# Order of the first loads, of the second unit's weight split and of the first gate recurrences in a hybrid block kernel

## The chip, the cores and the metric

The kernel runs on one core of a Trainium2 chip. The metric is the device time of one execution in microseconds (us), as a median of runs. A core has five engines with a queue of instructions each, executed in order: TensorE (PE, with its weight loads shown apart as PEld), VectorE (DVE), ScalarE (ACT), GpSimd (POOL) and SyncE (SP), which here issues nearly all transfers (DMAs).

## What is computed

One layer of a hybrid block on 16 meta tokens and 2048 tokens of width 1024, all in float32:

```python
h = concatenate([meta, x])                       # 2064 x 1024
p = rms_norm(h, norm_mix_pre) @ w_in             # 1024 -> 512 + 1544 + 1024 columns
oa = rg_lru_group(...)                           # a gated linear recurrence
ob = forgetting_attention_group(q, k, v, f_logit, fox_f_bias)
oc = rwkv7_group(...)                            # a matrix-valued recurrence
h = h + rms_norm(concatenate([oa, ob, oc]) @ w_out, norm_mix_post)
f = causal_dwconv(rms_norm(h, norm_ffn_pre) @ ffn_up)
h = h + rms_norm((gelu(gate) * val) @ ffn_down, norm_ffn_post)
```

The attention's decay comes from eight gate columns of p: `log_f = log_sigmoid(f_logit + f_bias)` and `c = cumsum(log_f)` along the tokens. That cumulative sum is the gate recurrence of the title.

## The kernel before

Each float32 product is made of three matmuls on rounded parts: an operand x becomes hi (rounded by ACT) and lo = x - hi (by DVE), and `mm3` (lines 185 to 189) adds hi*hi, hi*lo and lo*hi. So weights and tokens alike pass through a cast on ACT and a subtraction on DVE before PE can use them.

The input projection goes first. `w_in_part` (L334) takes the tokens in three parts of two blocks each; the first block of the first part has 400 tokens (the 16 meta tokens and three tiles of 128), the second 384 (three tiles). `w_in_norm` (L202) calls `norm_transpose` (L133) for each tile: a load on SP (L137), the sum of squares on ACT (L124), a scalar on DVE (L127), its power -0.5 on POOL (L128), the product with the reciprocal root and the norm's scale `g_pre` on DVE (L142), then eight transposes on PE into two PSUM tiles `pst` (L155), a cast to `xh` on ACT (L161) and a subtraction to `xl` on DVE (L162) for each. In the first part the second block's tiles are turned between the first units' products (`core.turn_tile`).

A unit is 128 output columns. Its weights (`wh`, `wl`) are loaded raw and split: L239 to L241 for the first two units, L177 to L182 for the others; two units' weights fit at a time (pool `w`), and the halves are stored (L250) for the later parts. For a block a unit costs 24 matmuls into one PSUM tile `psp`, evacuated by ACT (L58) or DVE (L60) to `stp` and stored (L277). Ahead of the units come the eight gate columns, 16 matmuls for a block into `psf` (L323, L324), evacuated at L326 and L328 and stored to `scr_f` (L329).

`gate_block` (L445) reads `scr_f` back (L457) and makes the cumulative sum: Abs, Exp and Ln on ACT (L459 to L461, with loads of ACT's function table between), DVE steps and the scan (L462 to L470), a cast on ACT (L475), a subtraction on DVE (L476) and two stores (L477, L478). It is the first step of `recurrences` (L2177), which a helper (`Beside`) advances between the units from the fourteenth unit on. The gated recurrences of the other two groups follow it, then attention, the output projection, and the up and down projections of the feed-forward.

The kernel is written in program order, and a scheduler sets the order of each engine's queue from priorities and its own model of time. `tc.issue_after(ins)` is an order edge: the instructions traced in its block stand behind `ins` on `ins`'s engine, with no semaphore. So code that stands late in the program can come early in a queue: the first `gate_block` stands behind thirteen units in the program, and its first load was placed right behind the store of `scr_f`.

Of the kernel before, what the change touches and what calls it, by code (L numbers as in the profile page):

```python
# [8 lines left out]
F32 = mybir.dt.float32  # L9
# [4 lines left out]
ALU = mybir.AluOpType  # L14
# [4 lines left out]
P = 128  # L19
# [13 lines left out]
class Core:  # L33


    def __init__(self, tc, ctx):
        self.tc = tc
        self.nc = tc.nc
        self.ctx = ctx
        self.uid = 0  # L40
        nc = self.nc
        self.const = ctx.enter_context(tc.tile_pool(name="const", bufs=1))
        self.ident = self.const.tile([P, P], F32, name="ident")
        make_identity(nc, self.ident[:])
        self.flip = 0
        self.root = self.apart = False
        self.power = None
        self.turns = 0

    def n(self, s):  # L50
# [79 lines left out]
    return rstd_from(core.nc, v, ss, width, core.apart)  # L130


def norm_transpose(core, pools, psum, src, rows, gain, pieces, after=nullcontext):  # L133

    nc = core.nc
    xt = pools["nt"].tile([P, D], F32, tag="nt_x", name=core.n("xt"))
    nc.sync.dma_start(xt[:rows], src)  # L137
    junk = pools["st"].tile([P, D], BF16, tag="stv", name=core.n("xj"))
    v = pools["nt"].tile([P, 6], F32, tag="rs", name=core.n("rs"))
    with after():  # L140
        rs = rstd_of(core, v[:rows], xt[:rows], D, junk[:rows])
    nc.vector.scalar_tensor_tensor(xt[:rows], xt[:rows], rs, gain[:rows], op0=ALU.mult, op1=ALU.mult)  # L142
    transpose_split(core, psum, xt, rows, pieces)


def transpose_split(core, psum, xt, rows, pieces):

    nc = core.nc
    for k0 in range(0, KD, 4):
        ps = psum.tile([P, 4, P], F32, tag="mm", name=core.n("pst"))
        for k in range(4):
            nc.tensor.transpose(  # L155
                ps[:, k, :rows], xt[:rows, (k0 + k) * P : (k0 + k + 1) * P], core.ident[:rows, :rows]
            )
        ks = slice(k0, k0 + 4)
        for hi, lo, c, r0, n in pieces:
            ds_, ss_ = slice(c, c + n), slice(r0, r0 + n)  # L160
            nc.scalar.activation(hi[:, ks, ds_], ps[:, :, ss_], AF.Copy)  # L161
            nc.vector.tensor_tensor(lo[:, ks, ds_], ps[:, :, ss_], hi[:, ks, ds_], op=ALU.subtract)  # L162


def split_load(core, pool, raws, src, shape, tag):
# [65 lines left out]
    return scr["wk"][c0 // P]  # L231


def w_in_weights(core, pools, w_in, c0, scr, part, raw=None):

    src = w_in[:, c0 : c0 + P].rearrange("(k p) c -> p k c", p=P)
    if raw is not None:
        pair = hi, lo = [pools["w"].tile([P, KD, P], F32R, tag=s, name=core.n(s)) for s in ("wh", "wl")]
        core.loaded = core.nc.sync.dma_start(raw, src)  # L239
        core.rounded = core.nc.scalar.activation(hi[:], raw, AF.Copy)  # L240
        core.nc.vector.tensor_tensor(lo[:], raw, hi[:], op=ALU.subtract)  # L241
    elif part == 0:
        pair = split_load(core, pools["w"], (pools["nt"], "nt_x", None), src, [P, KD, P], "w")
    else:
        core.turns += part == 2
        pl, tags = (pools["nt"], ("nt_x", "nt_x")) if core.turns % 4 > 1 else (pools["w"], ("wh", "wl"))
        pair = [pl.tile([P, KD, P], F32R, tag=tag, name=core.n(s)) for s, tag in zip(("wh", "wl"), tags)]
    for t, kept in zip(pair, w_in_kept(scr, c0)):
        t = t[:].rearrange("p k c -> p (k c)").bitcast(F32)
        core.loaded = core.nc.sync.dma_start(*((kept, t) if part == 0 else (t, kept)))  # L250
    return pair
# [82 lines left out]
def w_in_part(core, pools, psum, w_in, blocks, scr, part):  # L334
# [12 lines left out]
    if part == 0:  # L347
        raws = pools["rp"].tile([P, 2, KD, P], F32, tag="rw_e", name=core.n("raw"))
        firsts = [
            (w_in_weights(core, pools, w_in, c0, scr, part, raws[:, i]), kind, c0)  # L350
            for i, (kind, c0) in enumerate(units[:2])
        ]
        for i, block in enumerate(blocks):
# [91 lines left out]
def gate_block(core, R, f_bias, scr, tl):  # L445
# [8 lines left out]
        return R.t([NH, 400], s, dt)[:, :n]  # L454

    x = new("k")
    nc.sync.dma_start(x, scr["f"][:, t0 : t0 + n])  # L457
    a = new("r")
    nc.scalar.activation(a, x, AF.Abs, bias=core.fb[:])  # L459
    nc.scalar.activation(a, a, AF.Exp, scale=-1.0)  # L460
# [1741 lines left out]
def hybrid_block_kernel(ctx: ExitStack, tc: tile.TileContext, args, out):  # L2202
# [12 lines left out]
    def pool(es, name, bufs, **kw):  # L2215
        return es.enter_context(tc.tile_pool(name=name, bufs=bufs, **kw))
# [11 lines left out]
    with ExitStack() as p1:  # L2228
# [7 lines left out]
        rp = pool(rec, "rp", 1, **right)  # L2236
        with ExitStack() as p1a:
            ps_mm = pool(p1a, "ps_mm", 5, space=PSUM)
            g_pre = spread(pool(p1a, "gpre", 1), a["norm_mix_pre"], "g_pre")
            pools = {"xn": pool(p1a, "xn", 1), "nt": pool(p1a, "nt", 4), "w": pool(p1a, "w", 2), "st": pool(p1a, "st", 2)}  # L2240
            pools["us"], pools["rp"] = pool(p1a, "us", 1), rp
            sums = up_sums(core, pools["us"], a["ffn_up"], scr, EARLY)
            split_out = w_out_split(core, pools["nt"], a["w_out"], scr)
            core.power = core.const.tile([P, 1], F32, name="power")
            nc.vector.memset(core.power[:], -0.5)
            following = w_in_norm(core, pools, ps_mm, x, meta, g_pre, 0)
            for part in range(3):
                blocks = following
                units = w_in_part(core, pools, ps_mm, a["w_in"], blocks, scr, part)
                for i in range(READY if part == 0 else 0):  # L2250
                    while not next(units):
                        pass
                    if i == 4:
                        begun = core.loaded.ins
                if part == 0:
                    zeros = pools["st"].tile([P, PAD], F32, tag="sth", name="zeros")
                    nc.vector.memset(zeros[:], 0.0)
# [4 lines left out]
                        attn_consts(core)  # L2262
                    shared, core.const = core.const, rc
                    p1c = ExitStack()
                    p1c.enter_context(tc.issue_after(begun))
# [238 lines left out]
```

## Time and profile before

| | |
|---|---|
| median of 3 runs | 2953.49 us (2950.68 to 2956.22) |
| the profiled execution | 2962.62 us, its span 2960.9 us |
| PE busy | 2844.5 us, 96% of the span |
| DVE, ACT, POOL busy | 2002.2, 1505.8, 1297.3 us |
| mean granted TensorE clock | 0.976 |

The profile shows one execution, so sums are made against its own 2962.62 us. Times in it are microseconds from the start of the span. "Idle before <- releaser" is the time in which an engine had nothing to run, and what ended it. Tile names carry no numbers there; in listings of the program's order they do.

### The profile page before, as it was taken

Reading aid. Unit: us, or ns where it says so; the run is one execution under the profiler, and the core shown is the slowest. Engines: PE = TensorE matmul, PEld = TensorE weight load, DVE = VectorE, ACT = ScalarE, POOL = GpSimd, SP = SyncE. Lnnn points to the kernel's source line nnn. Section 1 sums busy time; section 2 is a strip of 40 time slices with the busy share of each in tenths; the row PEclk is TensorE's granted clock in tenths of the full one; section 3 lists DMA queues with packets and bytes.
Section 4 is the critical chain, followed back from the end, with each engine's and each line's share of the span. In section 5 each row is a group of like instructions: output and inputs, shape, how many; then the busy total and the mean of one; then the engine's idle time right before and its main releaser. Section 6 shows DMA issues by size and latency. Waiting matters only on the chain.

```text
span 2960.9 us, 53225 instructions
## 1 busy us (share of the span) xinstructions
PE 2844.5 (96%) x18854; PEld 2448.4 (83%) x18854; DVE 2002.2 (68%) x3839; ACT 1505.8 (51%) x2937; POOL 1297.3 (44%) x1572
## 2 busy tenths in 40 slices
PE   7998999999978889999999999999999999999998
PEld 7997989989865555566578999999999999787887
DVE  4257654666578765556656998888777787646766
ACT  4236442554346655555635666666566665324333
POOL 1002221222114667666723667355655544656443
PEclk9999999999988999999999999999999999999999
DMA  6776678577653357435255665577777774436453
GB/s 218 248 245 203 198 249 290 166 245 234 203 126 73 87 127 222 108 102 139 58 158 173 209 188 174 164 234 207 215 202 224 218 197 141 146 116 218 149 171 121
DMA packets 470343, 530.51 MB, mean 179 GB/s; under 512 B 86862, under 2 KB 356888, under 8 KB 468524
## 3 DMA queue, kind: packets, MB, share of 16 engines
q1 hardware_dynamic: 469308, 526.18, 58.9%
q8 instruction: 148, 2.42, 0.3%
q0 software_dynamic: 768, 0.93, 0.1%
q14 instruction: 119, 0.97, 0.1%
HBM read 368.07 MB, written 158.90 MB: 178 GB/s over the span
## 4 chain that ended last, share of the span: by engine, by line
PE 69%; DVE 7%; ACT 6%; DMA 5%; issue 2%; POOL 2%; SPq 1%; DVEq 0%; ACTq 0%; POOLq 0%
PE psu L187 9%; PE psu L188 9%; PE psu L189 9%; PE po L779 4%; PE psd L187 4%; PE psd L188 4%; PE psd L189 4%; PE psp L187 2%; PE psp L189 2%; PE psp L188 2%; PE sc L756 2%; PE mx L627 2%; PE sc L757 2%; PE pswo L187 2%; PE pswo L188 2%
## 5 line engine op out<-in xcount | busy, mean ns | idle before, releaser
L188 PE MATMUL psu<-xo,uw 128*128 128x344 f32 x1848 | 591.5, 320 | 0.0
L187 PE MATMUL psu<-xo,uw 128*128 128x344 f32 x1848 | 585.8, 322 | 3.3 <-ACT u L1933 2.3
L189 PE MATMUL psu<-xo,uw 128*128 128x344 f32 x1848 | 582.0, 320 | 0.3 <-DVE uw L1762 0.2
L187 PE MATMUL psp<-xh,wh 128*128 128x384 f32 (+2 forms) x1152 | 383.0, 333 | 0.4 <-DVE rww L1462 0.3
L188 PE MATMUL psp<-xl,wh 128*128 128x384 f32 (+2 forms) x1152 | 378.3, 328 | 0.0
L189 PE MATMUL psp<-xh,wl 128*128 128x384 f32 (+2 forms) x1152 | 375.6, 326 | 0.0
L1762 DVE TENSOR_TENSOR uw<-uq,uw 128x512 fp32r<-128x512 f32 x341 | 319.0, 940 | 60.6 <-ACT uw L1761 57.5
L187 PEld LDWEIGHTS psu<-xo,uw 128*128 128x128 f32 x1848 | 345.8, 188 | 4.8 <-ACT u L1933 2.6
L188 PEld LDWEIGHTS psu<-xo,uw 128*128 128x128 f32 x1848 | 347.1, 188 | 0.0
L189 PEld LDWEIGHTS psu<-xo,uw 128*128 128x128 f32 x1848 | 345.7, 188 | 1.2 <-DVE uw L1762 1.1
L1761 ACT ACTIVATE uw<-uq 128x512 fp32r<-128x512 f32 x462 | 288.1, 627 | 98.1 <-PE psu L189 41.1
L761 ACT ACTIVATE p<-sc,bias 128x512 f32<-128x512 f32 (+4 forms) x352 | 196.8, 590 | 164.3 <-PE sc L757 134.9
L632 DVE TENSOR_REDUCE mc<-mx 128x1 f32<-128x512 f32 (+5 forms) x352 | 191.8, 565 | 113.6 <-PE mx L627 83.7
L1901 DVE SCALAR_TENSOR_TENSOR uy<-psu,ffn_cols,uy 128x342 f32<-128x342 f32 (+1 forms) x390 | 220.5, 567 | 61.1 <-ACT uy L1899 59.7
L1909 POOL TENSOR_TENSOR uy<-uy,uy 128x342 f32<-128x342 f32 (+1 forms) x132 | 145.8, 1105 | 230.6 <-DVE uy L1901 58.4
L1762 POOL TENSOR_TENSOR uw<-uq,uw 128x512 fp32r<-128x512 f32 x121 | 183.3, 1515 | 133.7 <-ACT uw L1761 111.5
L187 PEld LDWEIGHTS psp<-xh,wh 128*128 128x128 f32 x1152 | 220.4, 191 | 7.7 <-issue 4.4
L188 PEld LDWEIGHTS psp<-xl,wh 128*128 128x128 f32 x1152 | 220.5, 191 | 5.6 <-issue 3.9
L189 PEld LDWEIGHTS psp<-xh,wl 128*128 128x128 f32 x1152 | 220.3, 191 | 4.3 <-issue 3.0
L800 POOL TENSOR_TENSOR acc<-acc,p 128x512 f32<-128x512 f32 (+3 forms) x186 | 196.4, 1059 | 49.8 <-DVE acc L800 22.2
L1762 DVE TENSOR_TENSOR fo<-u,fo 128x896 fp32r<-128x896 f32 x88 | 102.0, 1159 | 130.0 <-ACT fo L1761 129.4
L1761 ACT ACTIVATE fo<-u 128x896 fp32r<-128x896 f32 x88 | 81.2, 923 | 205.9 <-PE psd L189 118.3
(492 smaller groups left out, 6289.8 us busy)
## 6 DMA issues: line engine op xcount, KB each, us to landing
uq<-scr_us SPq DMA_DIRECT2D x220, 256.0 KB
uq<-in_ffn_up_dram SPq DMA_DIRECT2D x209, 256.0 KB
wl<-scr_wk SPq DMA_DIRECT2D x48, 512.0 KB
wh<-scr_wk SPq DMA_DIRECT2D x48, 512.0 KB
u<-scr_ff SPq DMA_DIRECT2D x88, 256.0 KB
scr_ff<-uy SPq DMA_DIRECT2D x110, 171.0 KB
raw<-in_w_in_dram SPq DMA_DIRECT2D x24, 512.0 KB
scr_wk<-wh SPq DMA_DIRECT2D x24, 512.0 KB
```

The costliest lines, as they stand in the source:

```text
L187: nc.tensor.matmul(out, ah, bh, start=first, stop=False, skip_group_check=more)
L188: nc.tensor.matmul(out, ah, bl, start=False, stop=False, skip_group_check=more)
L189: nc.tensor.matmul(out, al, bh, start=False, stop=last, skip_group_check=more)
L627: nc.tensor.matmul(ps[:rows, : e - a], q3[:, qo : qo + rows], k2[:, a:e], start=True, stop=not last)
L632: self.reduced = nc.vector.tensor_reduce(mc[:rows, i, ci : ci + 1], ps[:rows, : e - a], axis=AX.X, op=ALU.max)
L761: last = nc.scalar.activation(p[:rows, :w], ps[:rows, :w], AF.Exp, bias=bias[:rows, j : j + 1])
L779: mm = nc.tensor.matmul(po[at : at + 64, c0:n], v1[:rows, j], p[:rows, : n - c0], start=start and i < 2, stop=end and i + 2 >= len(group), ...
L800: eng.tensor_tensor(a, ps_[0][0][:rows, c0:n] if start and i == 1 else a, p[:rows, : n - c0], op=ALU.add)
L1761: core.nc.scalar.activation(hi, src, AF.Copy)
L1762: (eng or core.nc.vector).tensor_tensor(lo, src, hi, op=ALU.subtract)
L1901: core.conved = stt(y[:, :n], src[:, i : n + i], cw[:, 44 * i + cc : 44 * i + cc + 1], y[:, :n], op0=ALU.mult, op1=ALU.add)
L1909: core.pooled = nc.gpsimd.tensor_tensor(v[:, :n], g[:, :n], v[:, :n], op=ALU.mult)
```

## The change

It has three parts. The loads of the meta tokens and of the first full tile are issued ahead of the load of `g_pre`: they are kept in `core.held`, from which `norm_transpose` takes them. The second unit's cast and subtraction are put behind the last `xh` cast and the last `xl` subtraction traced before them (`core.high`, `core.low`), which are those of the first block's last tile. And the load of `gate_block` is put behind `core.begun`, the last store of weights traced in the fifth turn (i = 4) of the first part's loop; that name held the constants' edge before, as `begun`.

```diff
-        self.power = None
+        self.power, self.held = None, []
...
+def token_load(core, pools, src, rows):
+
+    xt = pools["nt"].tile([P, D], F32, tag="nt_x", name=core.n("xt"))
+    core.nc.sync.dma_start(xt[:rows], src)
+    return xt
...
 def norm_transpose(core, pools, psum, src, rows, gain, pieces, after=nullcontext):
-    xt = pools["nt"].tile([P, D], F32, tag="nt_x", name=core.n("xt"))
-    nc.sync.dma_start(xt[:rows], src)
+    xt = core.held.pop(0) if core.held else token_load(core, pools, src, rows)
...
-            nc.scalar.activation(hi[:, ks, ds_], ps[:, :, ss_], AF.Copy)
-            nc.vector.tensor_tensor(lo[:, ks, ds_], ps[:, :, ss_], hi[:, ks, ds_], op=ALU.subtract)
+            core.high = nc.scalar.activation(hi[:, ks, ds_], ps[:, :, ss_], AF.Copy)
+            core.low = nc.vector.tensor_tensor(lo[:, ks, ds_], ps[:, :, ss_], hi[:, ks, ds_], op=ALU.subtract)
...
-def w_in_weights(core, pools, w_in, c0, scr, part, raw=None):
+def w_in_weights(core, pools, w_in, c0, scr, part, raw=None, behind=False):
-        core.rounded = core.nc.scalar.activation(hi[:], raw, AF.Copy)
-        core.nc.vector.tensor_tensor(lo[:], raw, hi[:], op=ALU.subtract)
+        with core.tc.issue_after(core.high.ins) if behind else nullcontext():
+            core.rounded = core.nc.scalar.activation(hi[:], raw, AF.Copy)
+        with core.tc.issue_after(core.low.ins) if behind else nullcontext():
+            core.nc.vector.tensor_tensor(lo[:], raw, hi[:], op=ALU.subtract)
...
-            (w_in_weights(core, pools, w_in, c0, scr, part, raws[:, i]), kind, c0)
+            (w_in_weights(core, pools, w_in, c0, scr, part, raws[:, i], i > 0), kind, c0)
...
     x = new("k")
-    nc.sync.dma_start(x, scr["f"][:, t0 : t0 + n])
+    with core.tc.issue_after(core.begun):
+        nc.sync.dma_start(x, scr["f"][:, t0 : t0 + n])
...
-            g_pre = spread(pool(p1a, "gpre", 1), a["norm_mix_pre"], "g_pre")
+            gpre = pool(p1a, "gpre", 1)
...
+            core.held = [token_load(core, pools, meta, META), token_load(core, pools, x[:P, :], P)]
+            g_pre = spread(gpre, a["norm_mix_pre"], "g_pre")
             following = w_in_norm(core, pools, ps_mm, x, meta, g_pre, 0)
...
                     if i == 4:
-                        begun = core.loaded.ins
+                        core.begun = core.loaded.ins
```

What the edges do to the queues is read from the program's order (line, operation, tiles with their numbers, shape; the lines of the changed kernel are higher by 6 to 11). DVE's queue in the opening, before: `pst_165` to `pst_216` belong to the first block's three full tiles, `wl_232` and `wl_239` to the first and second unit, `fw` to the gate columns.

```order
L142 SCALAR_TENSOR_TENSOR xt_201<-xt_201,rs_204,g_pre 128x1024
L241 TENSOR_TENSOR wl_232<-raw_230,wh_231 128x1024
L162 TENSOR_TENSOR xl_132<-pst_165,xh_131 128x4x128
L241 TENSOR_TENSOR wl_239<-raw_230,wh_238 128x1024
L162 TENSOR_TENSOR xl_132<-pst_172,xh_131 128x4x128
L315 TENSOR_TENSOR fw_223<-fraw_224,fw_223 128x8x8
L162 TENSOR_TENSOR xl_132<-pst_187,xh_131 128x4x128
L127 TENSOR_SCALAR rs_298<-rs_298 128x1
L162 TENSOR_TENSOR xl_132<-pst_194,xh_131 128x4x128
L162 TENSOR_TENSOR xl_132<-pst_209,xh_131 128x4x128
L162 TENSOR_TENSOR xl_132<-pst_216,xh_131 128x4x128
```

The same place of DVE's queue in the changed kernel:

```order
L168 TENSOR_TENSOR xl_136<-pst_165,xh_135 128x4x128
L148 SCALAR_TENSOR_TENSOR xt_201<-xt_201,rs_204,g_pre 128x1024
L249 TENSOR_TENSOR wl_232<-raw_230,wh_231 128x1024
L168 TENSOR_TENSOR xl_136<-pst_172,xh_135 128x4x128
L168 TENSOR_TENSOR xl_136<-pst_187,xh_135 128x4x128
L168 TENSOR_TENSOR xl_136<-pst_194,xh_135 128x4x128
L127 TENSOR_SCALAR rs_298<-rs_298 128x1
L323 TENSOR_TENSOR fw_223<-fraw_224,fw_223 128x8x8
L168 TENSOR_TENSOR xl_136<-pst_209,xh_135 128x4x128
L168 TENSOR_TENSOR xl_136<-pst_216,xh_135 128x4x128
L148 SCALAR_TENSOR_TENSOR xt_295<-xt_295,rs_298,g_pre 128x1024
L249 TENSOR_TENSOR wl_239<-raw_230,wh_238 128x1024
```

`wl_239` has moved from the middle to behind the last `xl` and the next tile's product; the first tile's `xl` has moved ahead of the last tile's product. On ACT, `wh_238` moved likewise, and the square of the fifth tile (`xt_295`) now stands ahead of the casts of `pst_209` and `pst_216`.

ACT's queue at the second block's tiles (`pst_303` to `pst_382`), before, with the first gate's operations on `rwr_1343` and `rwk_1352`:

```order
L161 ACTIVATE xh_133<-pst_310 128x4x128
L459 ACTIVATE rwr_1343<-rwk_1341,fb 8x400
L460 ACTIVATE rwr_1343<-rwr_1343 8x400
L461 ACT_TABLE_LOAD
L461 ACTIVATE rwr_1343<-rwr_1343 8x400
L475 ACTIVATE rwk_1352<-rwsq_1349 8x400
L161 ACTIVATE xh_133<-pst_353 128x4x128
L161 ACTIVATE xh_133<-pst_360 128x4x128
L161 ACTIVATE xh_133<-pst_375 128x4x128
L161 ACTIVATE xh_133<-pst_382 128x4x128
L326 ACTIVATE fa_406<-psf_389 8x384
```

In the changed kernel those operations stand further on in ACT's queue, between the weights of the sixth unit (`wh_659`) and of the seventh (`wh_723`):

```order
L187 ACTIVATE wh_659<-raw_661 128x1024
L468 ACTIVATE rwr_1343<-rwk_1341,fb 8x400
L58 ACTIVATE stp_628<-psp_603 128x400
L469 ACTIVATE rwr_1343<-rwr_1343 8x400
L470 ACT_TABLE_LOAD
L470 ACTIVATE rwr_1343<-rwr_1343 8x400
L484 ACTIVATE rwk_1352<-rwsq_1349 8x400
L187 ACTIVATE wh_723<-raw_725 128x1024
```

The casts of `pst_353` to `pst_382` now follow that of `pst_310` directly. On SP the gate's load stands behind the store of `wh_659`; the second gate's operations moved from behind the third unit's weights to behind the seventh's. PE's order is the same in both programs up to the start of the attention.

More of the change, by code (lines that the diff above doesn't have):

```diff
@@ L2264, in hybrid_block_kernel @@
                     p1c = ExitStack()
-                    p1c.enter_context(tc.issue_after(begun))
+                    p1c.enter_context(tc.issue_after(core.begun))
                     p1c.enter_context(tc.issue_after(core.powered.ins))
```

## The prediction

> **What bounds the kernel now.** I began with the head of the page: TensorE (PE) is busy nearly throughout, so a gain has to be time in which PE waits or runs on a slow clock.
>
> ```profile
> span 2960.9 us, 53225 instructions
> PE 2844.5 (96%) x18854; PEld 2448.4 (83%) x18854; DVE 2002.2 (68%) x3839; ACT 1505.8 (51%) x2937; POOL 1297.3 (44%) x1572
> ```
>
> Then the busy time by stretches. A row gives start:end and length, then busy us (and instructions) of PE, PEld, DVE, ACT, POOL, then the granted TensorE clock, the DMA share and GB/s.
>
> ```profile
> 36.76:38.63 1.87, 0.00 (x1) 0.00 (x0) 1.87 (x5) 1.87 (x5) 0.00 (x0) 1.00 0.16 52
> 39.20:42.30 3.10, 3.08 (x10) 2.70 (x9) 0.95 (x2) 0.00 (x0) 0.00 (x0) 0.50 1.04 268
> 42.60:200.00 157.40, 157.40 (x879) 153.94 (x879) 52.58 (x117) 47.84 (x79) 9.29 (x15) 1.00 0.76 249
> 900.00:1100.00 200.00, 175.55 (x1677) 112.20 (x1675) 149.76 (x424) 120.65 (x264) 119.52 (x193) 0.88 0.38 90
> 1700.00:2500.00 800.00, 799.90 (x5080) 799.20 (x5079) 648.71 (x1001) 504.60 (x994) 434.65 (x343) 1.00 0.67 197
> ```
>
> From 42.6 us PE is the bound without a gap, at full clock; so is the up projection at 1700 to 2500. Time can be won before 42.6 us, and whatever is won there reaches 200 us whole. The stretch at 900 to 1100, where attention runs beside the last recurrences, is the soft one: 24.45 us idle, mean clock 0.88. Third, what PE waits for in the first 75 us (waits in total, times, longest):
>
> ```profile
> PE pst L155 <- DVE xt L142: 9.1, 2, 8.9
> PE psf L323 <- ACT xh L161: 3.2, 2, 1.9
> PE psf L324 <- DVE xl L162: 0.6, 1, 0.6
> ```
>
> So the opening is bound by DVE and ACT, which norm, transpose and split the tokens; PE follows them.
>
> **First tokens ahead of the norm's scale.** The timeline of the opening (start, length, engine, line, tiles, and in brackets the idle time before and its releaser):
>
> ```profile
> 0.81 0.39 SPq L2223 DMA_DIRECT2D g_pre<-in_norm_mix_pre_dram  x1
> 5.53 1.05 ACT L124 ACTIVATE xj<-xt 16x1024 bf16<-16x1024 f32 x1 [3.44 <-DMA xt<-in_meta_tokens_dram]
> 7.54 1.27 DVE L142 SCALAR_TENSOR_TENSOR xt<-xt,rs,g_pre 16x1024 f32<-16x1024 f32 x1 [0.56 <-POOL rs L128]
> 7.99 1.06 ACT L124 ACTIVATE xj<-xt 128x1024 bf16<-128x1024 f32 x1 [1.31 <-DMA xt<-in_x_dram]
> 9.34 1.06 ACT L124 ACTIVATE xj<-xt 128x1024 bf16<-128x1024 f32 x1 [0.21 <-DMA xt<-in_x_dram]
> 9.99 1.28 DVE L142 SCALAR_TENSOR_TENSOR xt<-xt,rs,g_pre 128x1024 f32<-128x1024 f32 x1 [0.67 <-POOL rs L128]
> ```
>
> The squares of the first two full tiles follow their loads and start 9.34 - 7.99 = 1.35 us apart: one 512 KB transfer. The scale g_pre is as large, so with it behind, the meta tokens and the first tile land about 1.35 us earlier. But L142 reads the scale too, and that now lands where the first tile used to, near 7.9. So the meta tile's L142 moves from 7.54 to about 7.95 (later), and the first tile's follows 1.27 us behind at 9.2 in place of 9.99: 0.75 us earlier. The third and fourth tiles do not land sooner, since the bytes ahead of them are the same. I take 0 for this edit alone; its ends are -0.4 (the later scale) and +0.75 us.
>
> **Second unit's weights behind the first block's tiles.** What PE's dense work waits for:
>
> ```profile
> 16.32 1.22 DVE L241 TENSOR_TENSOR wl<-raw,wh 128x1024 fp32r<-128x1024 f32 x1
> 18.84 1.87 DVE L162 TENSOR_TENSOR xl<-pst,xh 128x512 fp32r<-128x512 f32 x3
> 20.17 0.70 PE L324 MATMUL psf<-xl,fw 128*128 128x400 f32 x1 [0.55 <-DVE xl L162]
> ```
>
> The first L324 needs xl of all four tiles; PE goes on without a gap once it starts at 20.17. DVE is busy for 10.23 of the 10.7 us ahead of it,
>
> ```profile
> 10.00:20.70 10.70, 6.65 (x28) 5.11 (x29) 10.23 (x17) 9.21 (x19) 1.65 (x3) 0.91 1.00 292
> ```
>
> so an operation taken out of its queue shows in full. The second unit's L241 (1.22 us) goes behind the last xl, and its L240 (ACT) behind the last xh. Against it, the square of the fifth tile now stands ahead of the last two xh, which costs ACT one square (1.06 us) at about the price of the cast that left. The weights are first used when the second unit starts, some ten microseconds later; that is their cover. Gain 1.2 us, ends 0 (ACT becomes the later one) and 2.0 (with the 0.75 above).
>
> **First gates' recurrence behind unit five.** Around the second block's tiles:
>
> ```profile
> 30.32 0.28 SPq L457 DMA_DIRECT2D rwk<-scr_f  x1
> 31.86 0.63 ACT L459 ACTIVATE rwr<-rwk,fb 8x400 f32<-8x400 f32 x1 [0.53 <-DMA rwk<-scr_f]
> 33.08 1.28 ACT L461 ACT_TABLE_LOAD   x1
> 34.85 1.91 PE L155 MATMUL pst<-ident,xt 128*128 128x128 f32 x16
> 36.62 0.54 ACT L475 ACTIVATE rwk<-rwsq 8x400 fp32r<-8x400 f32 x1 [1.71 <-DVE rwsq L470]
> 37.06 2.00 ACT L161 ACTIVATE xh<-pst 128x512 fp32r<-128x512 f32 x4
> 37.68 2.47 DVE L162 TENSOR_TENSOR xl<-pst,xh 128x512 fp32r<-128x512 f32 x4
> 38.63 0.44 PE L323 MATMUL psf<-xh,fw 128*128 128x384 f32 x1 [1.87 <-ACT xh L161]
> 39.60 0.69 PE L324 MATMUL psf<-xl,fw 128*128 128x384 f32 x1
> 42.62 0.34 PE L189 MATMUL psp<-xh,wl 128*128 128x384 f32 x1
> ```
>
> The four xh casts stand behind L475 on ACT, which waits for the scan on DVE. PE's sixteen transposes end at 36.76, and PE idles 1.87 us. Without the gate on ACT the casts follow the transposes: the first group of four is there at 34.85 + 1.91/4, about 35.4; the casts are 0.5 us apart (2.00/4), so the third, for which L323 waits, ends near 36.9 and L323 starts near 37.0. Then xl is late next: 0.62 apart (2.47/4) on DVE, the third ends near 38.0, where L324 stood at 39.60. That is 1.6 us; I take 1.5, ends 0 and 1.87.
>
> The second part is the clock. It was 1.00 while PE idled and 0.50 in 39.20 to 42.30. From 39.60 to 42.62 PE started nine matmuls in 3.02 us; at the pace of the next stretch (157.40 / 879 = 0.179 us each) they take 1.61. The wait left over is a few tenths, so I count the slow stretch as gone: 1.4 us, ends 0 and 1.4.
>
> [...]
>
> ```profile
> 11.33 1.57 PEld L155 LDWEIGHTS pst<-ident,xt 128*128 128x128 f32 x8 [1.54 <-DVE xt L142]
> 16.45 0.42 PEld L155 LDWEIGHTS pst<-ident,xt 128*128 128x128 f32 x4 [0.81 <-DVE xl L162]
> ```
>
> **The gate's new place.** Its load now stands on SP behind the store of the sixth unit's wh, and L459 on ACT behind that cast, ahead of one stp and the seventh unit's wh:
>
> ```profile
> 75.67 0.38 SPq L250 DMA_DIRECT2D scr_wk<-wh  x1
> 77.56 1.06 ACT L181 ACTIVATE wh<-raw 128x1024 fp32r<-128x1024 f32 x1 [2.40 <-PE psp L188]
> 86.15 1.06 ACT L181 ACTIVATE wh<-raw 128x1024 fp32r<-128x1024 f32 x1 [1.51 <-PE psp L188]
> 34.37 0.54 ACT L461 ACTIVATE rwr<-rwr 8x400 f32<-8x400 f32 x1
> 34.95 0.56 DVE L463 TENSOR_TENSOR rwk<-rwk,rwr 8x400 f32<-8x400 f32 x1 [2.01 <-ACT rwr L461]
> 35.55 1.04 DVE L470 TENSOR_TENSOR_SCAN rwsq<-ones,ctail,rwk 8x400 f32<-8x400 f32 x1
> 691.81 4.76 DMA rwk<-scr_f
> ```
>
> With the opening 4.1 us ahead, the load goes out near 72.0 and lands 1.5 later (30.32 to 31.86) at 73.5. Then in line: L459 0.63, a stp 0.5 (like an xh cast), an exponential 0.54 (like the logarithm L461), the table load 1.28, the logarithm 0.54, L463 and L470 on DVE 1.6, L475 0.54, the cast 1.06 and the seventh unit's wl 1.2: 81.4. PE starts that unit when it frees the slot for the next cast, 86.15 - 4.1 = 82.05. So it is covered by about 0.7 us, and I price it at nothing. If the load takes the 4.76 us that a later gate's load takes in the chain that ended last (the last row), PE waits 4.76 - 1.5 - 0.7 = 2.6 us, and perhaps again for the second gate: ends 0 and 5.2. On SP the store of scr_ch waits for L475, and behind it a store of p and of wh; their readers come much later.
>
> **Later orders.** On DVE, ACT and POOL the order is that of before from about 90 to 900 us. At 900 to 1100 it is shuffled by up to some tens of places on PE, and in the up projection by a few, where PE has no gap to lose. I count 0 for it, but its ends are wide:
>
> ```profile
> PE mx L627 <- DVE mc L632: 7.8, 8, 3.7
> ```
>
> That is the largest wait at 900 to 1100. One stall of its longest kind with a slow stretch as above is 3.7 + 1.4 = 5.1 us, in either direction.
>
> **Sum.** 0 + 1.2 + 1.5 + 1.4 + 0 + 0 = 4.1 us. The profiled execution took 2962.62 us (span 2960.9), so it becomes 2958.5. It lies 9.1 us above the median of the runs, 2953.49; the same difference kept, I predict 2949.4.
>
> **The rivals.** About 0.2% (5.9 us) is what a measurement of this kernel can tell from no change.
> - The shuffle at 900 to 1100 takes out a stall: 2949.4 - 5.1 = 2944.3. For it: 24.45 us of gaps, and a mean clock of 0.88. Against it: nothing in the change aims there.
> - The shuffle puts in stalls: slower than before by over 0.2% needs 4.1 + 5.9 = 10.0, so it decides from the second new stall: 2949.4 + 10.2 = 2959.6. Against it: DVE is free for 50 of the 200 us there, so that a delayed step finds room.
> - The gate is late at its new place: 2.6 us once, 5.2 twice, so 2952 to 2954.6. For it: ACT and SP are in order, and the cover is 0.7 us. Against it: SP issues four DMAs fewer ahead of that place (both L457, L477, L478), so the load may go out sooner.
> - The clock falls anyway in the second block's tiles, or is slow for longer in the first: 2949.4 + 1.4 = 2950.8. [...]
>
> That the change does less than it says is inside the forecast: the reordered loads alone bring nothing.
>
> **The numbers.** Forecast 0.46, stall out 0.30, stalls in 0.08, gate late 0.10, clock 0.06. Faster by over 0.2% is the second alone, 0.30; slower 0.08; the rest, 0.62, is within 0.2%. The range leaves out the stalls-in case (0.08) and, of the stall-out case, what takes out more than one stall (0.10): 2943.0 to 2955.5, whose upper end holds the late gate.
>
> **What would show it.** Right: the first L324 near 19 us, at most 0.5 us of wait ahead of the second block's first psf matmul, clock 1.00 from 30 to 75 us, PE without a gap to 200 us. Wrong: a wait of PE for wh or wl of the seventh or eighth unit, a slow clock near 37 us, or a PE idle time at 900 to 1100 that differs from 24.45 by more than 4.

## The result, and the profile after

| | before | after |
|---|---|---|
| median, first comparison (17 runs each) | 2956.20 us | 2950.38 us |
| ratio of the two, 95% interval | | 0.9979 [0.9970, 0.9988] |
| median, second comparison (17 and 6 runs) | 2957.34 us | 2947.33 us |
| ratio | | 0.9964 [0.9952, 0.9976] |
| the kernel before against itself (12 and 17 runs) | | 0.9995 [0.9984, 1.0005] |
| span of the profiled execution | 2960.9 us | 2952.2 us |

The changed kernel is faster, by 6.2 us (3.5 to 8.9) in the first comparison and by 10.6 (7.1 to 14.2) in the second (the ratio's distance from 1 times the median of before). The forecast was a gain of 4.1 us and a time of 2949.4 us, 1.0 us below the measured median. That the time is so close is partly luck: it started from 2953.49 us, a median of 3 runs, and the 17 runs of the first comparison have 2956.20. The two medians lie 5.8 us apart, 1.7 more than forecast, and the start was 2.7 us higher.

The head of the page of the profile after the change (called after from here on): PE's busy share is what it was.

```profile
span 2952.2 us, 53222 instructions
PE 2835.8 (96%) x18854; PEld 2442.6 (83%) x18854; DVE 1999.0 (68%) x3839; ACT 1504.8 (51%) x2937; POOL 1301.5 (44%) x1572
```

The busy time by stretches, in after. The granted clock (third number from the right) is 1.00 from 30 to 75 us, and PE has no gap from 42.6 to 200 us, as before the change. From 900 to 1100 us PE is busy for 176.95 us, little more than the 175.55 of before, at the same clock of 0.88.

```profile
16.34:19.75 3.41, 2.82 (x9) 2.71 (x10) 3.40 (x7) 3.41 (x6) 0.55 (x1) 0.50 1.01 388
30.00:75.00 45.00, 44.49 (x255) 43.91 (x253) 11.16 (x16) 11.55 (x17) 0.00 (x0) 1.00 0.68 210
42.60:200.00 157.40, 157.40 (x884) 153.79 (x883) 57.14 (x128) 50.93 (x86) 9.60 (x15) 1.00 0.78 255
900.00:1100.00 200.00, 176.95 (x1532) 113.27 (x1533) 145.92 (x421) 116.08 (x253) 118.75 (x191) 0.88 0.41 96
```

What PE waits for in after's first 75 us (total, times, longest). The wait of 1.9 us at the second block's first matmul of the gate columns (`psf <- ACT xh`) is 0.4 us now. At the first block's first matmul, which waited for xh before, PE now waits 2.1 us for `fw`, the gate columns' weights.

```profile
PE pst L161 <- DVE xt L148: 9.0, 3, 8.4
PE psf L331 <- DVE fw L323: 2.1, 1, 2.1
PE psf L331 <- ACT xh L167: 0.4, 1, 0.4
PE psf L332 <- DVE xl L168: 0.2, 1, 0.2
```

The timeline of after, in the opening and at the second block's tiles. The first tile's square is at 5.13 (before: 7.99), and its product follows that of the meta tokens without a gap (7.05, x2). The first matmul with xl (L332, in before L324) starts at 17.74 in place of 20.17; the prediction had it near 19. At the second block's tiles the casts (31.45) follow the transposes (30.81), and PE goes on at 33.08.

```profile
5.13 1.06 ACT L124 ACTIVATE xj<-xt 128x1024 bf16<-128x1024 f32 x1 [1.06 <-DMA xt<-in_x_dram]
7.05 2.47 DVE L148 SCALAR_TENSOR_TENSOR xt<-xt,rs,g_pre 16x1024 f32<-16x1024 f32 x2 [0.45 <-DMA g_pre<-in_norm_mix_pre_dram]
8.36 1.06 ACT L124 ACTIVATE xj<-xt 128x1024 bf16<-128x1024 f32 x1 [2.08 <-DMA xt<-in_x_dram]
16.93 0.67 PE L331 MATMUL psf<-xh,fw 128*128 128x400 f32 x1 [2.06 <-DVE fw L323]
17.74 0.54 PE L332 MATMUL psf<-xl,fw 128*128 128x400 f32 x1
...
30.81 1.91 PE L161 MATMUL pst<-ident,xt 128*128 128x128 f32 x16
31.45 2.07 ACT L167 ACTIVATE xh<-pst 128x512 fp32r<-128x512 f32 x4 [4.15 <-PE pst L161]
33.08 0.44 PE L331 MATMUL psf<-xh,fw 128*128 128x384 f32 x1 [0.36 <-ACT xh L167]
```

How far PE is ahead later on can be read from one row: the cast of the ninth unit's weights, which PE releases when it has done the seventh unit. The row of before is shown here, that of after is the last of the next block: PE is 94.74 - 87.83 = 6.91 us ahead.

```profile
94.74 1.06 ACT L181 ACTIVATE wh<-raw 128x1024 fp32r<-128x1024 f32 x1 [3.49 <-PE psp L188]
```

The first gate at its new place in after: its load is issued at 68.50 and used at 71.08, 2.6 us later. The rows below it are the seventh unit's cast and its wl, the eighth unit's wl and the ninth unit's cast.

```profile
68.50 0.34 SPq L466 DMA_DIRECT2D rwk<-scr_f  x1
71.08 0.63 ACT L468 ACTIVATE rwr<-rwk,fb 8x400 f32<-8x400 f32 x1 [7.95 <-DMA rwk<-scr_f]
76.51 1.04 ACT L187 ACTIVATE wh<-raw 128x1024 fp32r<-128x1024 f32 x1
77.58 1.23 DVE L188 TENSOR_TENSOR wl<-raw,wh 128x1024 fp32r<-128x1024 f32 x1 [0.39 <-ACT wh L187]
86.44 1.22 DVE L188 TENSOR_TENSOR wl<-raw,wh 128x1024 fp32r<-128x1024 f32 x1
87.83 1.06 ACT L187 ACTIVATE wh<-raw 128x1024 fp32r<-128x1024 f32 x1 [1.04 <-PE psp L194]
```

A unit takes 94.74 - 86.15 = 8.59 us (in before), so PE began the seventh at 87.83 - 8.59 = 79.24, and its wl was there at 78.81: 0.43 us of cover. PE began the eighth at 87.83, and its wl, behind the second gate, was there at 87.66: 0.17 us. Both are covered, but barely.

### The profile page after: what moved, and what is told of

Its sections match the earlier page's. It is cut to its first block, busy times and chain, and to the rows that moved or that the text cites. A ratio compares the mean times of both kernels' runs of the same rounds, so it can differ in the third digit from the quotient of the medians.

```text
span 2952.2 us, 53222 instructions
## 1 busy us (share of the span) xinstructions
PE 2835.8 (96%) x18854; PEld 2442.6 (83%) x18854; DVE 1999.0 (68%) x3839; ACT 1504.8 (51%) x2937; POOL 1301.5 (44%) x1572
## 4 chain that ended last, share of the span: by engine, by line
PE 68%; DVE 8%; DMA 6%; ACT 5%; issue 3%; POOL 2%; SPq 1%; DVEq 0%; POOLq 0%; ACTq 0%
PE psu L193 10%; PE psu L194 9%; PE psu L195 9%; PE psd L193 4%; PE psd L194 4%; PE psd L195 4%; PE po L788 4%; PE psp L193 2%; PE psp L195 2%; PE psp L194 2%; PE mx L636 2%; PE sc L765 2%; PE pswo L193 2%; PE pswo L194 2%; PE pswo L195 2%
```

## The experiments

The two profiles left questions. Was the first L332 sooner by 2.4 us, where 1.2 was forecast, because of the reordered loads? And was the shorter slow clock of the opening (3.4 us at 0.50 in after, 6.8 in before) the change or luck? Theory A in the expectations mostly says that each edit brings what the profile after shows at its place. Lines are those of the changed kernel (of before for the fills). The "lead" is how much sooner the same PE matmul starts than in the first profile of before: the median over those that start between 30 and 35 us, 100 and 120, and at the end (2900 to 2950). The slow clock is the time at 0.50 that the profile records before 30 us.

| profile | first L332 | slow clock in the opening | wait at second block's first psf | lead at 30 | at 100 | at the end |
|---|---|---|---|---|---|---|
| before | 20.17 | 6.8 | 1.87 | 0 | 0 | 0 |
| before, again | 19.30 | 3.4 | 1.84 | 1.8 | 1.8 | 9.7 |
| gate alone | 19.77 | 6.8 | 0.35 | 0.2 | 3.1 | 4.1 |
| before, transposes twice | 20.17 | 6.8 | 2.78 | 0.3 | -1.7 | 4.7 |
| before, transposes thrice | 19.74 | 6.8 | 2.04 | 0.5 | -1.6 | 5.6 |
| tokens alone | 18.91 | 6.8 | 3.71 | 1.4 | -1.2 | 1.3 |
| tokens alone, again | 18.75 | 3.4 | 3.38 | 2.3 | 0.6 | 1.3 |
| weights alone | 18.85 | 3.4 | 2.83 | 2.4 | 0.4 | 0.5 |
| weights alone, again | 19.17 | 3.4 | 3.10 | 1.9 | -0.5 | -3.2 |
| tokens and weights | 17.83 | 3.4 | 3.18 | 3.8 | 0.2 | 7.3 |
| after | 17.74 | 3.4 | 0.36 | 4.0 | 6.9 | 8.8 |
| after, again | 17.68 | 3.4 | 0.35 | 3.4 | 6.2 | 1.9 |
| after, gate a turn later | 17.76 | 0 | 0.35 | 4.8 | 7.7 | 0.2 |
| after, three more edits | 17.14 | 0 recorded (see there) | 0.36 | 5.1 | 8.0 | 4.4 |

**Reordered loads alone.** The other two edits taken out of the changed kernel:

```diff
-            (w_in_weights(core, pools, w_in, c0, scr, part, raws[:, i], i > 0), kind, c0)
+            (w_in_weights(core, pools, w_in, c0, scr, part, raws[:, i]), kind, c0)
...
-    with core.tc.issue_after(core.begun):
+    with nullcontext():
```

> The loads of the meta tokens and of the first tile ahead of the scale, and nothing else of the change. Theory A (from the profile after): with the scale's load first, every load behind it lands about 1 us later, so the reorder alone brings the second to fourth tile's loads forward by about 1 us and the first L332 (xl, gate columns) from 20.17 to 19.0-19.3; PE's lead over the kernel before at 100 to 200 us is about 1.0. Theory B (the prediction's): the bytes ahead of the later tiles are the same, so the second tile still lands near 9.25, the first L332 stays at 20.17 within 0.3 and the lead is 0. Either can have up to 1.6 us more or less from where the clock's slow stretch ends in this one execution.

And once more:

> The reordered loads alone, once more. So far the first matmul with xl of the gate columns started at 19.3 to 20.2 us in five profiles with neither of the two opening edits (mean 19.83), at 18.91 with the reordered loads alone, at 17.7 to 17.8 with both in four. Theory (the reordered loads are worth about 1 us, because the first full tile's product leaves DVE's queue before the queue is full): 18.7 to 19.1 again, and DVE busy for 2.8 us or more of 7 to 10 us. Rival (18.91 was one of the scatter of 0.9 us that the kernels with the scale first show): 19.3 or later. In both the gain is lost at the second block's tiles, where the gate is still on ACT: PE waits 2.5 us or more there.

Measured (one execution each, 2961.33 and 2961.37 us, too few to read a change of the time from): the first L332 at 18.91 and 18.75, where five profiles without the opening edits have 19.30 to 20.17, mean 19.83. So the reorder is worth 1.0 us there, not 0. The reason that Theory A gave (later tiles land about 1 us sooner) covers less than half of it: with the scale first, the second full tile's square starts between 8.09 and 9.44 (seven profiles, mean 8.93), with it behind between 8.36 and 8.68 (seven, mean 8.49): 0.4 us. The first full tile's product, which DVE makes ahead of all that, starts 1.4 us sooner: at 8.25 to 8.57 (mean 8.37) in place of 9.28 to 10.10 (mean 9.79). The windows of 7 to 10 us in before, before again and tokens alone again show this in DVE's column (the third busy time):

```profile
7.00:10.00 3.00, 1.03 (x8) 0.92 (x8) 1.43 (x3) 1.81 (x3) 1.07 (x2) 1.00 1.05 377
```
```profile
7.00:10.00 3.00, 1.03 (x8) 0.93 (x8) 2.06 (x3) 2.80 (x6) 0.80 (x2) 1.00 1.09 359
```
```profile
7.00:10.00 3.00, 1.39 (x10) 1.29 (x11) 2.76 (x5) 1.47 (x5) 0.10 (x2) 1.00 1.05 383
```

DVE did 0.7 to 1.3 us more ahead of 10.00, and from there on it is nearly full (7.5 to 7.7 of the 8 us from 10 to 18 in these three).

**Second unit's weights alone.** The loads in their old order, the gate's edge out as above:

```diff
-            gpre = pool(p1a, "gpre", 1)
+            g_pre = spread(pool(p1a, "gpre", 1), a["norm_mix_pre"], "g_pre")
...
-            core.held = [token_load(core, pools, meta, META), token_load(core, pools, x[:P, :], P)]
-            g_pre = spread(gpre, a["norm_mix_pre"], "g_pre")
...
-    with core.tc.issue_after(core.begun):
+    with nullcontext():
```

> Only the second unit's cast and subtraction behind the first block's last xh and xl. Theory A and the prediction agree: 1.22 us out of DVE's queue, the first L332 at 18.9-19.1 in place of 20.17, a lead of 1.2 at 100 to 200 us. Rival: ACT, which takes the fifth tile's square in place of the cast, or the late loads set the time, so that the first L332 comes less than 0.5 us earlier and the 2.43 us seen with all three edits need the reordered loads as well.

And once more:

> The second unit's weights behind the first block's tiles alone, once more: the first L332 at 18.85 in the first profile of it. Theory: 18.2 to 18.9, that is 1.0 to 1.2 less than the 19.3 to 20.2 of the kernels with neither opening edit, with their scatter, since the loads still begin with the scale; a slow clock of one stretch of 3.4 us in the opening; the gain lost at the second block's tiles, with a wait of 2.5 us or more. Rival: 19.3 or later, and 6.8 us of slow clock.

Measured (one execution each, 2962.05 and 2965.85 us): the first L332 at 18.85 and 19.17, mean 19.01, 0.8 less than 19.83; the second lies between what the theory and the rival expected. With the loads reordered too it is 17.75 (mean of the four), 1.1 less than with those alone. So the edit is worth 0.8 to 1.1 us there, in place of 1.2.

**Both, with the gate left on ACT.** Only the gate's edge is taken out of the changed kernel:

```diff
-    with core.tc.issue_after(core.begun):
+    with nullcontext():
```

> The changed kernel with the gate's load left where it was: tokens and weights alone. Theory A: the first L332 at 17.7-17.9 as in the changed kernel; the wait of 1.87 us for xh ahead of the second block's first psf matmul is back, within 0.4, and the slow clock of 0.50 behind it; lead at 100 to 200 us 2.4, or up to 4.0 if the clock's slow stretch of the opening ends early as it did in the profile after. Rival: the two opening edits do not add up (the first L332 at 18.5 or later), and part of the 6.9 us of lead at 200 us belongs to the gate.

Measured: 2953.47 us, ratio 0.9991 [0.9980, 1.0003]; the first L332 at 17.83, a lead of 3.8 us at 30 us, and of 0.2 at 100. That was expected by neither: the gate did not cost its 1.87 us, it took all that the opening had won.

```profile
28.16 0.43 SPq L466 DMA_DIRECT2D rwk<-scr_f  x1
31.08 1.91 PE L161 MATMUL pst<-ident,xt 128*128 128x128 f32 x16
31.64 0.63 ACT L468 ACTIVATE rwr<-rwk,fb 8x400 f32<-8x400 f32 x1 [4.09 <-DMA rwk<-scr_f]
34.63 0.54 ACT L470 ACTIVATE rwr<-rwr 8x400 f32<-8x400 f32 x1
35.07 1.52 ACT L167 ACTIVATE xh<-pst 128x512 fp32r<-128x512 f32 x3
36.17 0.44 PE L331 MATMUL psf<-xh,fw 128*128 128x384 f32 x1 [3.18 <-ACT xh L167]
```

And the slow clock behind it, by the windows of the same profile:

```profile
37.27:44.10 6.83, 6.14 (x19) 6.14 (x20) 1.79 (x5) 0.54 (x1) 0.00 (x0) 0.50 0.06 13
```

The transposes come 3.8 us sooner than in before (34.85), but the load of the gate is used at 31.64, as in before (31.86). With the weights moved, SP issues a store of p and a 512 KB load of weights ahead of the gate's load, and that is used 3.48 us after its issue (2.80 and 3.64 in the two profiles with the weights alone), in before 1.54. Three of the casts stand on ACT behind the gate's logarithm (34.63), so PE waits 3.18 us, and the slow clock behind that lasts 6.83 us in place of 3.41.

The same loss stands in all four profiles with one opening edit: leads of 1.4 to 2.4 us at 30 us fall by 1.7 to 2.6. With the tokens alone the reason is another one. Nothing stands between the store of scr_f and the load, as in before, but the load was issued 3.02 us behind the store, in before again 1.39:

```profile
27.57 0.29 SPq L337 DMA_DIRECT2D scr_f<-fo  x1
30.59 0.27 SPq L466 DMA_DIRECT2D rwk<-scr_f  x1
```
```profile
27.18 0.28 SPq L329 DMA_DIRECT2D scr_f<-fo  x1
28.57 0.28 SPq L457 DMA_DIRECT2D rwk<-scr_f  x1
```

Six profiles have this order on SP. The distance is 1.39 and 1.40 us in the two of before, 3.02 and 2.93 with the tokens alone, 3.08 and 3.34 in the two runs below that only repeat transposes; these two have neither opening edit and lose 2.0 to 2.1 us too. So what the tokens gained was eaten by a late load, and whether that comes of the edit or of chance is not shown.

**Gate alone.** The loads in their old order (as in the run of the weights alone), the weights' edges out, the gate's edge in; PE's order is that of before to the end.

```diff
-            (w_in_weights(core, pools, w_in, c0, scr, part, raws[:, i], i > 0), kind, c0)
+            (w_in_weights(core, pools, w_in, c0, scr, part, raws[:, i]), kind, c0)
...
-            core.held = [token_load(core, pools, meta, META), token_load(core, pools, x[:P, :], P)]
```

> Only the first gate's load behind the fifth turn's store of weights; PE's order is that of the kernel before from end to end. Theory A and the prediction: the first L332 stays at 20.17 within 0.3; the wait of the second block's first psf matmul falls from 1.87 to at most 0.5 us; the granted clock is 1.00 from 30 to 75 us; PE leads by 1.5 at 40 us and by 2.9 at 100 to 200 us, and since its order is the same, by about 2.9 at the end: a ratio near 0.999. Rival (gate late): PE waits 1 us or more for wh or wl of the seventh or eighth unit, which lessens the lead at 100 us. Rival (the lead was the clock's luck): the clock falls to 0.5 all the same, lead 1.5.

Measured: 2954.39 us, ratio 0.9989 [0.9975, 1.0002]; the wait is 0.35 us, the lead rises from 0.2 at 30 us to 3.1 at 100, by 2.9.

```profile
36.90 0.45 PE L331 MATMUL psf<-xh,fw 128*128 128x384 f32 x1 [0.35 <-ACT xh L167]
91.62 1.06 ACT L187 ACTIVATE wh<-raw 128x1024 fp32r<-128x1024 f32 x1 [1.64 <-PE psp L194]
```
```profile
30.00:75.00 45.00, 44.50 (x256) 43.91 (x255) 11.54 (x16) 10.14 (x17) 0.00 (x0) 1.00 0.67 207
```

This is the forecast's 1.5 + 1.4 to the tenth: wait and slow clock both go with the gate, and at the new place nothing is late. The single part does not show in the time, whose interval holds 1.

**Transposes in the gap.** The kernel before, with the seventh tile's transposes (the last of the second block) done three times, or twice, into the same place:

```diff
-        for k in range(4):
+        for k in [*range(4)] * core.again:
...
-        t0, _, _, hi, lo = block
+        (t0, _, tl, hi, lo), core.again = block, 3 if part == 0 and s == 656 else 1
```

> The kernel before, with the sixteen transposes of the sixth and seventh tile followed by sixteen more: each transpose of the seventh tile is done three times, into the same place, so that PE is busy with transposes where it idled for 1.87 us at the second block's tiles. The gate stays on ACT ahead of the casts, so that the first L323 of the second block is no sooner. Theory A (the clock fell because of the idle PE, and transposes hold it): the idle time is at most 0.4 us and the granted clock stays 1.00 from 36 to 42.6; PE's lead at 100 to 200 us is 1.0 to 1.4. [...]

> As the run with three, with each transpose of the seventh tile done twice: some 0.9 us of idle PE is left in place of 1.87. Theory A: half of the idle time is short enough, the clock stays 1.00 and PE leads by 1.0 to 1.4 at 100 to 200 us; if it falls all the same, an idle time of 0.9 us is already too long. [...]

Measured (one execution each, 2957.07 us with three and 2957.94 with two): the gap was not filled, since the gate came 1.4 us later in both than in the first profile of before (L459 at 33.3 in place of 31.86). So this tells nothing on how short a gap is harmless. But it shows what the clock did while PE ran transposes. With three:

```profile
34.37 3.65 PE L155 MATMUL pst<-ident,xt 128*128 128x128 f32 x32
40.07 0.44 PE L323 MATMUL psf<-xh,fw 128*128 128x384 f32 x1 [2.04 <-ACT xh L161]
```
```profile
35.21:38.62 3.41, 2.81 (x26) 2.57 (x24) 2.17 (x5) 1.70 (x4) 0.00 (x0) 1.00 0.25 74
34.37:41.90 7.53, 5.33 (x41) 4.76 (x40) 5.13 (x10) 4.39 (x8) 0.00 (x0) 1.00 0.48 121
42.03:45.45 3.42, 3.42 (x12) 3.42 (x12) 0.00 (x0) 0.00 (x0) 0.00 (x0) 0.50 0.85 232
```

From 34.37 to 40.07, 5.7 us, PE did nothing but transposes and 2.04 us of waiting, and the clock stayed at 1.00 until 42, when it fell for one stretch of 3.42 us. The changes of the clock lie on a grid of 3.41 us (last section), and one whole step of it, 35.21 to 38.62, holds 2.81 us of transposes and no other matmul; the clock did not fall at its end. In before, the step from 35.74 to 39.16 holds 1.87 us of waiting, and the clock fell at its end. The opening shows the same of transposes. In 13 of the 14 profiles (all but the one with three more edits) PE did nothing but transposes, 3.0 to 3.4 us of them, in the 3.41 us ahead of the first recorded clock of 1.00, and from that point on the weight load of a transpose takes 0.14 us in place of 0.23. In before that point is 15.26, and the two rows of transposes' weight loads that stand in the prediction lie on both sides of it: 1.57/8 = 0.20 us for each of eight at 11.33, 0.42/4 = 0.105 for each of four at 16.45 (less than the length of one, since they overlap). So in 13 profiles the clock came to 1.00 behind transposes alone, and in the run with three it stayed there for a step that held no other matmul.

**Gate one turn later.** The edge is taken from the sixth turn's store; PE's order is that of after.

```diff
-                    if i == 4:
+                    if i == 5:
```

> The changed kernel with the first gate's load one turn later, behind the sixth turn's store of weights; PE's order is that of the changed kernel from end to end. Theory A: the gate still fits under one unit's products (8.6 us), by a few tenths of a us; no wait of PE between 42.6 and 200 us, lead 6.9 at 100 to 200 us. Rival: at the new place the load lands later than 2.5 us and PE waits 0.5 to 3 us for wh or wl of the eighth unit. As PE's order is the same, the time of its second block's tiles and the length of the opening's slow clock show how much of the 6.91 is repeated: the waits are, the slow clock of 3.4 us could be 6.8 (a lead 1.4 to 1.6 lower).

Measured: 2962.40 us (one execution), no wait of PE from 42.6 to 200 us, lead 7.7 at 100 us.

```profile
82.29 1.23 DVE L188 TENSOR_TENSOR wl<-raw,wh 128x1024 fp32r<-128x1024 f32 x1 [0.39 <-ACT wh L187]
95.59 1.06 ACT L187 ACTIVATE wh<-raw 128x1024 fp32r<-128x1024 f32 x1 [3.54 <-PE psp L194]
```

The eighth unit's wl is there at 83.52, and PE begins that unit at 95.59 - 8.59 = 87.00: 3.5 us of cover in place of 0.43 for the first gate, so the few tenths that I expected were wrong too. A turn later would be the safer place.

**Three more edits in the opening.** On top of after: a buffer of its own for the gate columns' raw weights, the fifth tile's square behind the last xh, and the first unit's wl behind the last xl:

```diff
-        raw = pools["st"].tile([P, KD, 8], F32, tag="stv", name=core.n("fraw"))
+        raw = pools["us"].tile([P, KD, 8], F32, tag="fraw", name=core.n("fraw"))
...
-        after = (lambda: core.tc.issue_after(core.rounded.ins)) if late else nullcontext
+        after = (lambda: core.tc.issue_after(core.rounded.ins)) if late else (lambda: core.tc.issue_after(core.high.ins)) if part == 0 and s == 400 else nullcontext
...
-        with core.tc.issue_after(core.low.ins) if behind else nullcontext():
+        with core.tc.issue_after(core.low.ins) if raw is not None else nullcontext():
```

> The changed kernel with three more edits: the gate columns' raw weights have a buffer of their own, so that their load is issued ahead of the two units' weights and not behind the fifth tile; the fifth tile's square stands behind the first block's last xh; and the first unit's wl, like the second's, behind the last xl. Theory (what is late next in the opening is fw, for which PE waits 2.06 us, and DVE): the first L331 at 15.3-15.9 in place of 16.93, the first L332 at 16.3-16.8 in place of 17.74, and PE leads the kernel before by 8.0 to 8.5 us at 100 to 200 us in place of 6.91; more by up to 1.6 if the shorter idle time lets the clock stay at 1.00. Rival: the first unit's wl is now late for its first use, and PE waits there for what was won. The later order changes at some places, worth plus or minus 5 us at the end as in the other runs; the ratio to the kernel before 0.996 to 0.998.

Measured: 2953.23 us, ratio 0.9990 [0.9973, 1.0006], so not shown to be better than after, nor than before. In the profile the opening did gain: the first L332 at 17.14 (expected 16.3 to 16.8), the wait for fw gone, lead 8.0. The profile gives a clock of 1.00 from 10 to 75 us, but its record begins only at 18.19, and the rows say that PE was slow until then: weight loads of the same matmuls take 0.33 us before it and 0.19 after.

```profile
14.53 1.94 PE L161 MATMUL pst<-ident,xt 128*128 128x128 f32 x8 [0.71 <-DVE xt L148]
16.31 0.70 PE L331 MATMUL psf<-xh,fw 128*128 128x400 f32 x1
17.14 0.59 PE L332 MATMUL psf<-xl,fw 128*128 128x400 f32 x1
17.87 0.33 PEld L331 LDWEIGHTS psf<-xh,fw 128*128 128x128 f32 x1
18.20 0.19 PEld L332 LDWEIGHTS psf<-xl,fw 128*128 128x128 f32 x1
```

So two things were late. PE waited 0.71 us for the last tile's product on DVE, and the eight transposes of that tile then took 1.94 us, where after has 1.07 (at 13.81, at the full clock). In the other 13 profiles the first clock of 1.00 is recorded ahead of the first matmul of the gate columns.

**Both kernels once more, unedited.**

> The changed kernel once more, unedited. Theory A (what the change brings is made before 45 us: 2.4 us sooner dense work, a shorter slow clock ahead of the second unit, no wait and no slow clock at the second block's tiles): first L332 at 17.5-17.9, slow clock of at most 3.5 us in the opening, none at 30 to 75, PE's lead over the first profile of before 6.9 to 8.0 at 100 to 200 us; behind that, with the same order as the first profile of the changed kernel, the lead wanders by up to 5 us either way between 600 and 1200 us. Rival (the shorter slow clock of the opening was luck): 6.8 us of slow clock there, lead 5.2-5.5. Ratio 0.997 to 0.999.

> The kernel before once more, unedited: a measure of what two runs of one program differ by. Ratio 1.000 within 0.001. Theory A: 6.8 us of slow clock in the opening again (as in the five kernels whose second unit's weights were not moved); the first gate's load lands 1.5 to 4 us behind its issue, so that the wait of the second block's first psf matmul is anywhere between 1.8 and 3.7 us, and PE's place at 100 us differs from the first profile's by 0 to -2 us. Rival: the first profile was typical, the wait is 1.9 within 0.3 and the place the same within 0.3. The lead at 600 to 1200 us wanders by several us although the order is the same.

Measured: the ratios of the table at the top. The slow clock of the opening was 3.4 us in this profile of before, where the theory had 6.8; the first one, from which I predicted, was one of the long ones. PE's lead at 100 us is 6.9 and 6.2 in the two of after (the second below the expected 6.9 to 8.0), 7.7 with the gate a turn later, and 0 and 1.8 in the two of before. The means differ by 6.9 - 0.9 = 6.0 us. The first comparison of the runs measured 6.2 us; the second measured 10.6 (7.1 to 14.2), and what it has above 6.0 is not explained. Behind 100 us one execution tells nothing: between there and the end the second profile of before gains 8.0 us on the first, and the second of after loses 6.2 on the first of after. At 900 to 1100, before again and after again:

```profile
900.00:1100.00 200.00, 180.44 (x1640) 116.13 (x1640) 149.32 (x429) 118.52 (x259) 122.44 (x198) 0.88 0.42 99
```
```profile
900.00:1100.00 200.00, 177.24 (x1608) 115.12 (x1608) 145.13 (x416) 116.63 (x253) 117.26 (x193) 0.86 0.39 91
```

## Why the prediction was right, and where not

- **Tokens ahead of the scale: 0.** This step failed: it is worth 1.0 us at the first L332. That later tiles land hardly sooner was nearly right (0.4 us). What failed is "I take 0": the prediction had found the first tile's product 0.75 us earlier, and DVE full behind it, but did not join the two. On the engine that bounds the stretch, work done ahead of the full stretch counted here nearly like work taken out (0.7 to 1.3 us more of DVE's work ahead of 10.00, 1.0 us at the first L332). The 0.75 was too small as well. The first tile did not land 1.35 us earlier, as one transfer less ahead of it would give: its square starts 2.5 us earlier and its product 1.4 (means of seven profiles each). Its claim that the meta tile's product comes later fell as well: it starts at 7.05 to 7.37 in the seven profiles with the new order, at 7.09 to 7.83 in the seven with the old one; the scale landed before 7.4, not near 7.9.
- **Second unit's weights: 1.2.** Right in mechanism, slightly too large: 0.8 to 1.1 at the first L332. What the prediction did not see is that the same edit puts a 512 KB load ahead of the gate's load on SP: with the gate in its old place, the gate's load was then used 2.80 to 3.64 us after its issue (three profiles), in before 1.54.
- **The slow clock of the opening.** No term of the sum had it. It lasted 6.8 us in four of five profiles with neither opening edit, 3.4 in three of the four with both, 0 in the other: on average 6.1 and 2.6 us at half speed, so about 1.8 us are won. Part of that is luck, for with the tokens alone, and in before itself, it was 6.8 us in one profile and 3.4 in the other. What goes with the length is how much of PE's last waits falls into the first slow stretch of 3.41 us: PE was busy for 2.82 us or more of it in the seven profiles where the clock then came back, for 2.41 to 2.86 in the five where it stayed slow for a second stretch. That sooner weights and tokens shorten those waits is my estimate and not shown (2.79 us in before, 2.82 in after); where the stretch begins differs from one execution of a program to the next (18.68 in before, 20.41 in before again).
- **Gate off ACT: 1.5 + 1.4.** Right: 2.9 with the gate alone, 2.9 in after. But the sum took the three edits as independent, and "whatever is won there reaches 200 us whole" did not hold with the gate left on ACT: there 3.8 us of lead became 0.2. Added up, the leads of the single edits at 100 us are -0.3 (mean of tokens alone), -0.1 (of weights alone) and 3.1, in all 2.7 us; together they give 6.2 to 6.9.
- **The gate's new place: 0.** Right; no wait in the four profiles with the gate there, nor in the one with it a turn later. The load took 2.6 us, not 1.5, but was issued 3.5 us sooner than I had it (68.50 for 72.0).
- **The later order: 0.** Not refuted. One execution wanders by 5 us and more there with the order unchanged (before again gains 8 us on before between 700 and 1100 us), so a cost of the shuffle below that can't be told.

The rivals with stalls put in and with a late gate did not come; the clock did not fall at the second block's tiles. A gain of over 0.2%, to which I gave 0.30 by way of a stall taken out, is what the second comparison shows and the first leaves open. The profiles show 6.0 us, or 0.2%, of it in the opening. They show no stall taken out at 900 to 1100: PE's idle time there is 24.45 and 19.56 us in the two of before, 23.05 and 22.76 in the two of after. So the forecast's mechanism held for its largest part, the gate, and its size came out near the measured one although it left out 1.0 us of the tokens and some 1.8 us of clock.

## What to carry to other kernels

Ask of a gain ahead of a wait whether the end of that wait moves too. If it hangs on something else (here two small transfers, what stands ahead of them in their queue, and a chain on ACT), the gain may show only once the wait is gone, and single edits then add up to less than the whole (here 2.7 us of lead at 100 us against 6.2 to 6.9). On the engine that bounds a stretch, moving work to before the stretch can count like removing it (here 1.0 us at the first L332). Before a gain of a few microseconds is read from one profile, profile the same program twice: here two of the same program differed by 10 us at the end. And check a granted clock of 1.00 ahead of the first record by the length of like instructions on both sides of it (here weight loads of 0.33 and 0.19 us).

## What the hardware showed

- In the first 75 us the slow clock came in stretches of 3.41 us, or two of them, and its changes lie on a grid of that step (in before 15.26, 18.68, 25.50, 39.16 and 42.57), which starts at another point in each profile: 16.34 to 19.75 in after, 18.24 to 21.65 in after again, 18.68 to 25.50 in before. In before again the clock fell at 37.47 behind 1.84 us of waiting. In the steps of 3.41 us ahead of the falls in the first 75 us PE was busy for 0.79 to 1.98 us; three steps with 1.59 to 1.94 had no fall behind them, so a threshold is not shown.

```profile
18.24:21.65 3.41, 3.41 (x12) 3.37 (x11) 2.75 (x5) 2.17 (x5) 0.89 (x2) 0.50 1.08 369
```
```profile
18.68:25.50 6.82, 6.20 (x18) 5.56 (x18) 5.71 (x10) 2.42 (x5) 2.65 (x6) 0.50 1.05 388
```

- From the issue of a store of 12.5 KB to the issue of the load that waits for it took 1.39 and 1.40 us in two profiles and 2.93 to 3.34 in four others; the reason is open.
